# The hybrid mixers step on one Trainium2 core: two pauses of level four in the HGRN2 recurrence's place in the queue of jobs

## The chip, the core and the metric

The kernel runs on one core of one Trainium2 chip. A core has a matrix engine (TensorE, PE in the profile; PEld is its weight load), three engines for everything else (VectorE or DVE, ScalarE or ACT, GpSimd or POOL) and a queue that issues transfers (SyncE, SP). Each engine runs its own list of instructions in its own order; semaphores tie them together. Results of TensorE land in PSUM, which the others read.

The metric is the time of one execution on the device, in microseconds. The kernel before takes 1027.42 us, the median of three runs (1027.24 to 1028.08).

## The reference, cut to what matters

Two inputs, 512 sample tokens and 128 prompt tokens, go through one layer. The 640 tokens are normalised, multiplied by a wide matrix `w_in`, and the columns of the result feed four mixers side by side:

```python
h = rmsnorm(x, lw['norm1_g']) * (1.0 + sc1) + sh1
proj = h @ lw['w_in']
(a_x, a_b, a_c, b_q, b_ff, b_fb, b_i, b_g, c_q, c_k, c_v, d_u, d_v) = jnp.split(proj, IN_SPLITS, axis=-1)
y_a = a_b * dwconv3(a_c * a_x, lw['conv_a_w'], lw['conv_a_b'])
y_b, s_f, s_b = hgrn2_bidir(b_q, b_ff, b_fb, b_i, b_g, ...)
y_c = ...attention over a neighbourhood...
y_d = chunk_gmlp(d_u, d_v, ...)
merged = (g_a * (y_a @ lw['w_br_a']) + ... + g_d * (y_d @ lw['w_br_d']))
x = x + g1 * (merged @ lw['w_o'])
x = x + g2 * conv_ffn(rmsnorm(x, lw['norm2_g']) * (1.0 + sc2) + sh2, ...)
```

The change lies in `hgrn2_bidir`, a recurrence run forwards and backwards over the tokens. In one direction, with decay `f`, key `k`, value `v` and query `q`:

```python
decay = jnp.exp(jnp.where(tri, rel, -jnp.inf))
scores = jnp.einsum('bhctd,bhcsd,bhctsd->bhcts', q, k, decay)
o_intra = jnp.einsum('bhcts,bhcsv->bhctv', scores, v)
u = jnp.einsum('bhcsd,bhcsv->bhcdv', k * jnp.exp(cum_end - cum), v)
s_next = g_c[..., None] * s + u_c
o_inter = jnp.einsum('bhctd,bhcdv->bhctv', q * jnp.exp(cum), s_in)
```

## The kernel before

Features lie on the 128 partitions and the 640 tokens along the free axis. The projection by `w_in` is the backbone of the first third of the kernel. It goes section by section (the forget gates, q, i, g, dv, du, ck, cq, cv, ac, ax, ab), each in two tiles of 128 columns. One tile (`in_tile`, which calls `gemm`) is 48 matmuls of 128x320 in two halves of 8 groups; a group (one k) is three matmuls, because each product is made of a high and a low part. Each tile's weights are split into these parts by ScalarE (L323) and VectorE (L324) two tiles ahead.

The mixers' small work is put in between by a queue of jobs. It acts while the program is written out, not on the chip. A job is a generator; it issues instructions and yields a pause. A counter `now` stands for TensorE's time: each group of a projection tile adds 0.41 to it (`tick`), small products inside a job add their own estimate (`pe`), and after each tick every job that is due takes one step:

```python
def step(j):
    j[0] = now[0] + (next(j[1]) or 0.0) * j[2]
def tick(us):
    now[0] += us
    for j in list(jobs):
        if j[0] <= now[0]:
            step(j)
```

`j[0]` is the due time, `j[2]` a factor on the job's pauses: 1.3 for the recurrence, which starts when the q section is done. The list `HD` holds pauses of the jobs; `HD[1]` is 5. Python evaluates `now[0]` in `step` before it runs the job.

The order so written is TensorE's order in this region; the framework lays out the other engines' work around it from data dependencies and its own estimates, and sets all semaphores.

The recurrence (`hgrn`) doubles the length of the block in seven levels. At each of levels one to four it makes, for each half of the features (`par` 0 and 1), a burst of 40 small products (80 matmuls in the profile, since the operands are plain f32) into one bank of PSUM (L526). VectorE merges them under a mask (L531). After the first burst the job pauses (L537, 0.4); after the second it scales keys and queries for the next level (L545, L549), and pauses again (L550, `HD[1]`). At level four the merged scores are also copied to the large matrix `at` by ScalarE (L541). Level five has bursts of the same size and level six four smaller ones, and there ScalarE copies them (L535). Then follow, in the same job: the transposes of keys (`kt_load`, L565, L568), state updates (`upd`, L574, L585), outputs (L612 to L624), a pause for the norm, and five steps of last transposes (L635, L639).

Other jobs at work in this region: `ada_cols`, which makes the modulation's later columns on VectorE (L262), loads its weights by SyncE (L248), and has one transpose on TensorE after its eighth column (`gain_rows`, L291); `gmlp`, with five steps of 8 products (L673) and their scaling on VectorE (L678). All small products take their PSUM bank from a pool of four, `psm`.

Of the kernel before, what the change touches and what calls it, by code (L numbers as in the profile page):

```python
# [17 lines left out]
HD = [4, 5, 2.1, 7, 2.2, 1.4, 1.5, 5, 2.0, 2, 11]  # L18
# [49 lines left out]
def tile_step(ctx: ExitStack, tc: tile.TileContext, a: dict, outs: list, dbg=None):  # L68
# [21 lines left out]
    def pe(us):  # L90
        now[0] += us
# [38 lines left out]
    def pm():  # L130
        return psm.tile([P, 512], F32, tag="m", name=nm("m"))
# [315 lines left out]
    def hgrn():  # L447
# [13 lines left out]
        def along(x):  # L461

            m = pm()
            mv = m[:, 0:20].rearrange("p (r i) -> p i r", r=2)
            for i in range(10):
                mm(mv[:, i, :], x[:, i * P:(i + 1) * P], heads, start=True, stop=True)
                pe(0.22)
                yield 0.5
            return m
# [16 lines left out]
        def blk(x, B):  # L486
            return x.rearrange("p n t -> p (n t)").rearrange("p (n j i) -> p n j i", j=2, i=B)

        def keys(l):
            B = 1 << l  # L490
            kl = (he if l % 2 == 0 else hd)[:, 0:1280]
            klv = kl.rearrange("p (n j i) -> p n j i", j=2, i=B)
            vec.tensor_copy(klv[:, :, 0, :], blk(kk[:, 0], B)[:, :, 0, :])
            act(klv[:, :, 1, :], blk(kk[:, 1], B)[:, :, 1, :], AF.Copy)
            return kl
# [3 lines left out]
        for l in range(7):  # L499
            B = 1 << l  # L500
            e_, x_ = blk(kk[:, 0], B), blk(kk[:, 1], B)
            r_, p_ = blk(qq[:, 0], B), blk(qq[:, 1], B)
            f_, g_ = blk(ff[:, 0], B), blk(ff[:, 1], B)
            nb = 1280 // (2 * B)
            if l == 0:
                m = yield from along(near)
                vec.copy_predicated(nat, lmask[:, 0, :].unsqueeze(1).to_broadcast([P, 20, 32]), bc(m))

            W = 64 if l == 6 else 32
            ns = 320 // W  # L510
            for s0, par in ([(s_, r) for s_ in range(0, 10, ns) for r in range(2)] if l else ()):
                b = slice(64 * par, 64 * par + 64)
                m = pm()
                for i in range(s0, s0 + ns):
                    for g in range(P // W):
                        d, t0 = (0, W * g) if l < 5 else (1 - g % 2, W * (g ^ 1))
                        t0 += (i % 5) * P
                        k0 = i * P + W * g
                        rhs = qq[b, d, i // 5, t0:t0 + W]
                        if l < 5:  # L520
                            lhs = kl[b, k0:k0 + W]
                            rhs = bass.AP(rhs.tensor, rhs.offset,
                                          [list(rhs.ap[0]), [2 * B, 16 // B], [1280 + B, 2], [1, B]])
                        else:
                            lhs = f2(kk[:, g % 2])[b, k0:k0 + W]
                        mm(m[W * g:W * g + W, (i - s0) * W:(i - s0 + 1) * W], lhs, rhs,  # L526
                           start=True, stop=True, tile_position=(64 * par, W * g))
                    pe(0.18)
                mv = m[:, 0:ns * W].rearrange("p (i t) -> p i t", t=W)
                if l < 5:  # L530
                    vec.copy_predicated(near_at[:, par], lmask[:, l, :].unsqueeze(1).to_broadcast([P, 10, 32]), mv)  # L531
                else:
                    for g in range(P // W):
                        c = slice(W * g, W * g + W)
                        act(at[c, par, s0:s0 + ns, W * (g ^ 1):W * (g ^ 1) + W], mv[c], AF.Copy)  # L535
                if par == 0:
                    yield 0.4  # L537
            if l == 4:
                for g in range(4):
                    c = slice(32 * g, 32 * g + 32)  # L540
                    act(at[c, :, :, c].rearrange("p r i t -> p (r i) t"), nat[c], AF.Copy)  # L541
            ups = ((e_[:, :, 0, :], f_[:, :, 1, 0:1]), (x_[:, :, 1, :], g_[:, :, 0, 0:1]),
                   (p_[:, :, 1, :], f_[:, :, 0, 0:1]), (r_[:, :, 0, :], g_[:, :, 1, 0:1]))
            for i, (dst, mul) in enumerate(ups):
                vec.tensor_tensor(dst, dst, mul.to_broadcast([P, nb, B]), ALU.mult)  # L545
                if i == 1 and l < 4:
                    kl = keys(l + 1)
            fa = ff.rearrange("p d n t -> p (d n t)").rearrange("p (n j i) -> p n j i", j=2, i=B)
            vec.tensor_tensor(fa[:, :, 0, 0], fa[:, :, 0, 0], fa[:, :, 1, 0], ALU.mult)  # L549
            yield HD[1]  # L550
        vec.tensor_copy(tot, ff.rearrange("p d n (t s) -> p d n t s", s=P)[:, :, :, :, 0])
        R["tots"] = True

# [331 lines left out]

    SLACK = {"q": 1.3, "du": 1.4, "ax": 1.0, "cv": 1.1}
    starts = {"q": hgrn, "du": gmlp, "ax": conva, "cv": attn}

    def in_tile(sec, n, w):
# [1283 lines left out]
```

## Time and profile before

| | |
|---|---|
| median of three runs | 1027.42 us (1027.24 to 1028.08) |
| the profiled execution | 1028.79 us |
| its span, first to last instruction | 1026.9 us |
| TensorE busy | 1013.4 us (99%) |
| VectorE busy | 792.3 us (77%) |
| ScalarE busy | 535.5 us (52%) |
| mean granted TensorE clock | 0.996 |
| recurrence, levels one to six on TensorE (L526) | 110.5 to 157.3 us of the span |

Times in the profile count from the span's first instruction. The chain of waits follows the work that ended last back from the end: each of its rows has a start, a length and what it was; "issue" is time in which the engine waited for nothing that the profile shows. A count there can be below the number of matmuls issued, since neighbours that overlap are merged and a few records can be missing. In a row of the view by stretches stand the stretch, its length, the busy time and number of instructions of PE, PEld, DVE, ACT and POOL, the granted clock of TensorE, the share of the DMA engines and GB/s. In the list of waits: who waited, for whom, the total in us, how often, the longest. In the page's third part a row of a DMA queue has packets, MB, and share.

### The profile page before, as it was taken

The page shows a single profiled execution, that of the slowest core. Times are in us where ns is not written, and L with a number is a line of the kernel's source. Part 1 is how long each engine was busy: PE and PEld are TensorE (multiplying, and loading weights), DVE is VectorE, ACT ScalarE, POOL GpSimd, SP SyncE. Part 2 cuts the span into 40 slices and gives each one's busy share as a digit, 9 for nine tenths or more (in the row PEclk, how much of TensorE's full clock was granted, in tenths as well). Part 3 has the DMA queues.
Part 4 walks back from the last instruction along what each step waited for, and adds up shares of the span by engine and source line. Part 5 has one row for each costly group of instructions (what it writes and reads, how often), then busy time and mean ns, then how long its engine had stood idle before and what let it go on. Part 6 is the DMA issues. An engine that isn't in the chain of part 4 may idle for free.

```text
span 1026.9 us, 18833 instructions
## 1 busy us (share of the span) xinstructions
PE 1013.4 (99%) x7620; PEld 957.8 (93%) x7620; DVE 792.3 (77%) x1300; ACT 535.5 (52%) x927; POOL 106.2 (10%) x149
## 2 busy tenths in 40 slices
PE   8999999999999999999999999999999999999997
PEld 6899999999899999999998899999999999888886
DVE  6658889679965676767768879998888887797634
ACT  6642343444444444544544567777777776633332
POOL 1000010313100000000010111111112211001101
PEclk9999999999999999999999999999999999999999
DMA  9864333598562413323179584765555669974212
GB/s 354 319 220 127 125 108 121 137 270 268 121 205 78 137 69 103 127 79 103 41 276 359 200 333 109 192 167 150 149 150 149 156 161 274 366 248 149 89 35 103
DMA packets 55927, 177.87 MB, mean 173 GB/s; under 512 B 8192, under 2 KB 14624, under 8 KB 53280
## 3 DMA queue, kind: packets, MB, share of 16 engines
q1 hardware_dynamic: 45008, 140.60, 39.5%
q0 software_dynamic: 10832, 36.06, 14.7%
q8 instruction: 60, 0.98, 0.4%
q14 instruction: 27, 0.22, 0.1%
HBM read 134.93 MB, written 25.46 MB: 156 GB/s over the span
## 4 chain that ended last, share of the span: by engine, by line
PE 96%; DMA 1%; ACT 1%; DVE 1%; issue 1%; SPq 0%; POOL 0%; POOLq 0%; DVEq 0%; ACTq 0%
PE g L1464 19%; PE g L362 17%; PE m L1108 17%; PE g L1795 8%; PE m L1795 6%; PE g L1121 5%; PE m L1464 4%; PE m L1248 3%; PE g L920 2%; PE g L1248 2%; PE m L148 2%; PE g L148 1%; PE m L526 1%; PE m L1459 1%; DMA A<-in_w_ada_dram 1%; PE m L851 1%
## 5 line engine op out<-in xcount | busy, mean ns | idle before, releaser
L362 PE MATMUL g<-XH,w 128*128 128x320 f32 x704 | 171.9, 319 | 0.0
L362 PEld LDWEIGHTS g<-XH,w 128*128 128x128 f32 x704 | 121.6, 190 | 2.2 <-issue 1.2
L362 PE MATMUL g<-XL,w 128*128 128x320 f32 x352 | 109.8, 312 | 0.0
L362 PEld LDWEIGHTS g<-XL,w 128*128 128x128 f32 x352 | 66.9, 190 | 0.3 <-issue 0.2
L311 DVE TENSOR_TENSOR w<-raw,w 128x1024 fp32r<-128x1024 f32 x34 | 41.5, 1222 | 21.4 <-ACT w L310 15.2
L1108 PE MATMUL m<-XH,w 128*128 128x320 f32 x224 | 52.5, 309 | 0.0
L1795 PE MATMUL g<-w,XH 128*128 128x512 f32 (+1 forms) x216 | 47.6, 373 | 0.0
L310 ACT ACTIVATE w<-raw 128x1024 fp32r<-128x1024 f32 x34 | 35.7, 1050 | 21.3 <-PE g L1248 9.9
L1795 PEld LDWEIGHTS g<-w,XH 128*128 128x128 f32 x216 | 38.4, 188 | 7.6 <-ACT XH L1758 0.3
L148 DVE SCALAR_TENSOR_TENSOR X<-MG,p2t,X 128x641 f32<-128x641 f32 x44 | 38.9, 885 | 4.3 <-ACT X L148 3.4
L148 DVE SCALAR_TENSOR_TENSOR X<-X,p2t,X 128x641 f32<-128x641 f32 x44 | 38.9, 885 | 1.9 <-ACT X L148 1.0
L1795 PE MATMUL g<-w,XL 128*128 128x512 f32 (+1 forms) x180 | 39.8, 372 | 0.0
L148 ACT ACTIVATE w<-raw 128x1024 fp32r<-128x1024 f32 (+3 forms) x46 | 38.2, 850 | 2.9 <-DMA raw<-in_w_in_dram 2.0
L1795 PE MATMUL m<-w,XH 128*128 128x512 f32 (+1 forms) x180 | 39.7, 368 | 0.0
L1464 PE MATMUL g<-XL,w 128*128 128x320 f32 x240 | 38.6, 310 | 0.0
L1464 PE MATMUL g<-XL,C 128*128 128x320 f32 x240 | 38.4, 309 | 0.0
L1795 PEld LDWEIGHTS g<-w,XL 128*128 128x128 f32 x180 | 32.3, 188 | 6.5 <-DVE dt L1806 0.4
L1108 PEld LDWEIGHTS m<-XH,w 128*128 128x128 f32 x224 | 38.3, 188 | 0.0
L1464 PEld LDWEIGHTS g<-XL,w 128*128 128x128 f32 x240 | 36.0, 188 | 0.5 <-ACT MG L148 0.3
L1464 PEld LDWEIGHTS g<-XL,C 128*128 128x128 f32 x240 | 35.9, 188 | 0.4 <-ACT MG L148 0.4
L1795 PEld LDWEIGHTS m<-w,XH 128*128 128x128 f32 x180 | 31.3, 189 | 5.3
L1108 PE MATMUL m<-XL,w 128*128 128x320 f32 x112 | 34.6, 309 | 0.0
(546 smaller groups left out, 2764.5 us busy)
## 6 DMA issues: line engine op xcount, KB each, us to landing
raw<-in_w_up_dram SPq DMA_DIRECT2D x30, 512.0 KB, 5.2
raw<-in_w_gp_dram SPq DMA_DIRECT2D x21, 640.0 KB, 3.9
raw<-in_w_down_dram SPq DMA_DIRECT2D x22, 512.0 KB, 4.0
raw<-in_w_in_dram SPq DMA_DIRECT2D x19, 512.0 KB, 4.1
H<-in_w_adt_dram SPq DMA_DIRECT2D x16, 512.0 KB, 4.3
actd<-X POOLq DMA_DIRECT2D x22, 320.5 KB, 5.5
X<-in_w_adt_dram SPq DMA_DIRECT2D x10, 512.0 KB, 4.4
upd<-XL SPq DMA_DIRECT2D x4, 1280.0 KB, 6.5
```

The costliest lines, as they stand in the source:

```text
L148: r = f(*args, **kw)
L310: act(w[0], raw, AF.Copy)
L311: vec.tensor_tensor(w[1], raw, w[0].bitcast(F32), ALU.subtract)
L362: mm(o, w[:, h, k0 + k, :], r(k)[:, s], start=(k == 0 and i == 0), stop=(k == kt - 1 and i == 2))
L526: mm(m[W * g:W * g + W, (i - s0) * W:(i - s0 + 1) * W], lhs, rhs, start=True, stop=True, tile_position=(64 * par, W * g))
L851: mm(mo[64 * hh_:64 * hh_ + 64, 0:P], v, ptt[(u + hh_) % 3][:, j * P:(j + 1) * P], start=(j == 0), stop=(j == 2))
L920: mm(o, x(kx)[:, ts], w[:, h, k, :], start=(kx == 0 and i == 0), stop=(kx == 7 and i == 2))
L1108: mm(o, w[:, k, :], x[:, k, :], start=(first and k == 0 and j == 0), stop=(k == 3 and j == 2), skip_group_check=True)
L1121: mm(pb[:, c, 0:HC], w[:, h + k, :], y[:, x, k, s], start=(k == 0 and j == 0), stop=(k == 1 and j == 2))
L1248: mm(m, mh[k // 2][:, hx, k % 2, t * P:(t + 1) * P], wo[q][:, hw, k % 2, :], start=(k == 0 and i == 0), stop=(k == 7 and i == 2))
L1464: z = mm(o, w[:, k, :], x[:, k, :], start=(first and k == 0 and j == 0), stop=(k == 3 and j == 2), skip_group_check=True)
L1795: mm(acc[nh][t + c0 // 256][:, 0:c1 - c0], sl[k][hx][:, t * P:(t + 1) * P], w[:, hw, k, c0:c1], start=(kk_ == 0 and k == 0 and i == 0), st ...
```

## The change

At level four the pause after the first burst becomes 1.6, and the closing pause becomes 5 - 1.2 = 3.8. All other levels keep 0.4 and 5. No instruction is added, removed or altered in what it computes.

```diff
                 if par == 0:
-                    yield 0.4
+                    yield 1.6 if l == 4 else 0.4
...
             vec.tensor_tensor(fa[:, :, 0, 0], fa[:, :, 0, 0], fa[:, :, 1, 0], ALU.mult)
-            yield HD[1]
+            yield HD[1] - (1.2 if l == 4 else 0)
```

## The prediction

> **What bounds the kernel now.** I read the page's engine shares and instruction queue first, then the waits of TensorE, the chain of waits around the level, and a table of busy time by stretch.
>
> ```profile
> span 1026.9 us, 18833 instructions
> PE 1013.4 (99%) x7620; PEld 957.8 (93%) x7620; DVE 792.3 (77%) x1300; ACT 535.5 (52%) x927; POOL 106.2 (10%) x149
> q8 instruction: 60, 0.98, 0.4%
> ```
>
> TensorE (PE) is busy for 1013.4 of 1026.9 us, so another engine's order matters only where it makes PE wait. All PE waits of the kernel that the view lists:
>
> ```profile
> PE g L148 <- DVE F L148: 1.6, 1, 1.6
> PE m L148 <- DMA A<-in_w_ada_dram: 1.3, 2, 0.9
> PE m L526 <- issue: 1.1, 1, 1.1
> PE m L148 <- DVE X L148: 1.1, 4, 0.3
> PE m L1464 <- DVE w L148: 0.4, 1, 0.4
> PE m L1464 <- ACT MG L148: 0.3, 1, 0.3
> ```
>
> One of these, 1.1 us, lies in L526, the recurrence's bursts. The chain of waits from level three to the end of the recurrence's levels (start, length, what):
>
> ```profile
> 128.35 0.82 PE m L526 x58
> 129.17 5.47 PE g L362 x36
> 134.64 0.82 PE m L526 x58
> 135.46 0.21 PE m L291
> 135.67 0.44 PE g L362 x3
> 136.11 0.75 PE m L526 x54
> 136.86 1.14 issue
> 138.00 0.26 PE m L526 x7
> 138.26 7.01 PE g L362 x36
> 145.27 0.82 PE m L526 x58
> 146.09 0.64 PE g L362 x3
> 146.73 0.82 PE m L526 x58
> 147.55 5.47 PE g L362 x36
> 153.02 0.73 PE m L526 x20
> ```
>
> Level four is the pair at 134.64 and 136.11. Its second burst stops for 1.14 us near its end, where PE waits for nothing shown. Afterwards 36 projection matmuls take 7.01 us where the same 36 take 5.47 us after levels three and five: 1.54 us more. The stretches tell why (length, PE busy, ..., granted clock):
>
> ```profile
> 135.00:138.40 3.40, 2.26 (x137) 1.88 (x126) 3.02 (x8) 0.27 (x1) 0.00 (x0) 1.00 0.20 41
> 138.40:141.80 3.40, 3.40 (x14) 3.40 (x14) 3.37 (x7) 2.90 (x4) 0.00 (x0) 0.50 0.35 125
> 141.80:205.00 63.20, 63.20 (x682) 60.34 (x681) 51.18 (x106) 26.64 (x60) 11.86 (x11) 1.00 0.41 121
> ```
>
> For 3.4 us after the stop the granted clock is 0.50. So in this execution the stop costs 1.14 + 1.54 = 2.68 us. From 141.80 to 205.00 PE has no idle time and the full clock.
>
> That stop looks like an instruction fetch: 7620 matmuls and 7620 weight loads over 60 packets are 254 instructions a packet, and over 134.0 to 136.8 us the DMA view has one packet only, one of these:
>
> ```profile
> DMA packets 1, 0.02 MB, mean 6 GB/s; under 512 B 0, under 2 KB 0, under 8 KB 0
> q8 instruction: 1, 0.02, 2.2%
> ```
>
> A level's two bursts are 80 matmuls each, so 320 instructions: more than one packet. In level four, two packet ends are only 2 us apart: the stop comes 146 instructions into the second burst (73 matmuls), so the end before it lies 254 - 146 - 8 = 100 instructions from the close of the first burst.
>
> [...]
>
> **The change part by part.** The edit moves no instruction by itself: it alters two due times in the queue of jobs that decides where the recurrence's steps are put among the projection's matmuls. A step's due time is the counter before the step plus pause times 1.3 (the slack of the job started at "q"). A burst adds 10 x 0.18 = 1.8 to the counter; each group of three projection matmuls adds 0.41 and then lets due jobs run.
>
> 1. The pause of 1.6. Before: due 0.4 x 1.3 = 0.52 after the first burst began. After: 1.6 x 1.3 = 2.08. But the burst itself moves the counter by 1.8, and the first chance to run is at 1.8 + 0.41 = 2.21 (level four has the gain transpose there too, 0.11 more). Both due times are past by then. The second burst stays where it is, after three matmuls. The row 135.67 (x3) is this rule at work, and so is 146.09. So the program up to the end of level four's second burst is unaltered, and with it the packet ends: the stop of 1.14 us and the slow 3.4 us stay. Change: 0.
>
> 2. The closing pause. It counts from the start of the second burst. Before: 5 x 1.3 = 6.5; less 1.8, 4.7 remain, which is 12 groups (12 x 0.41 = 4.92): the 36 matmuls of rows 129.17, 138.26 and 147.55. After: 3.8 x 1.3 = 4.94; less 1.8, 3.14 remain: 8 groups (3.28). Level five's first burst comes 4 groups, 12 matmuls, earlier. A group is 0.44 us, from
>
> ```profile
> 323.45 1.76 PE g L1121 x12
> ```
>
> (0.147 us each), so 1.76 us: 145.27 becomes about 143.5. It pulls everything that follows in this job: level six, the state updates, the outputs.
>
> Does its data come in time? Level five reads what level four's updates leave, and level six what level five's leave (timeline of VectorE):
>
> ```profile
> 138.73 1.55 DVE L545 TENSOR_TENSOR C<-C,A 128x640 f32<-128x640 f32 x2
> 140.19 0.30 DVE L549 TENSOR_TENSOR A<-A 128x80 f32<-128x80 f32 x1
> 149.57 1.56 DVE L545 TENSOR_TENSOR C<-C,A 128x640 f32<-128x640 f32 x2
> 160.56 0.60 DVE L678 SCALAR_TENSOR_TENSOR X<-m,cst,G 128x128 f32<-128x128 f32 x2
> 161.08 1.22 DVE L262 SCALAR_TENSOR_TENSOR junk<-X,S 128x1024 bf16<-128x1024 f32 x1
> 162.22 1.13 DVE L678 SCALAR_TENSOR_TENSOR X<-m,cst,G 128x128 f32<-128x128 f32 x4
> ```
>
> For level five they end at 140.5: 3 us of cover are left. For level six they end at 151.1 against a burst at 153.0; its distance from level five's second burst stays 12 groups, and these updates now stand ahead of a weight split that VectorE did first. Cover about 1.9 us, taken as enough; if one 1.22 us operation (row 161.08) still gets ahead, it is used up and nothing more.
>
> New packet ends: counted from the stop, 14 instructions of level four are left, then 24 matmuls (48), 160 of level five's first burst and 6, so the next end is 26 instructions into its second burst, about 145.1 us, some 7 us after the stop; one more 254 on is the start of level six's second burst, about 152.6. No two come within 2 us. Change: 0.
>
> 3. Breaks in the stream. 36 matmuls take 5.47 us after a burst, against 36 x 0.147 = 5.28: each return to the projection costs 0.19 us. Stepping the queue by hand with the two due times, the recurrence's and the gMLP's steps from here on interrupt the projection at 22 places instead of 21 (before the last transposes, whose 5 stay): level six's later bursts no longer share a place with the gMLP's first two steps, while the first state transpose now shares one with its last. Change: +0.19 us, between 0 and +0.4 if one place more or less falls together.
>
> 4. The far end. The chain's last transposes run during the last cv tile, 2.46 counter units earlier; attention and the rest start only when that tile is done. From tile ac on the order is as before. Change: 0.
>
> Semaphores, DMA issues and the amount of work on each engine are unaltered. SyncE's queue keeps its loads; the weight loads released by VectorE's splits may move by the length of a few operations, with two tiles (over 10 us) of cover.
>
> Sum: 0 + 0 + 0.19 + 0 = +0.2 us, a span of 1027.1. The profiled execution took 1028.79, 1.37 above the runs' median of 1027.42; against the median the forecast is **1027.6 us**. 0.2% (2.05 us) is about the least that a measurement of this kernel tells from no change.
>
> **The rivals.**
>
> (B) The pause does separate the bursts. That would be so if the due time counted from the end of the burst: 2.08 is 6 groups, 18 matmuls. Then the second burst starts some 5 x 0.44 = 2.2 us later, its packet has come, and the stop and the slow stretch both go: 1027.6 - 2.68 = 1024.9. Against it: by that count 0.52 would need two groups, 6 matmuls, and all rows have 3.
>
> [...]
>
> (C) Slower. PSUM's pool for small results has four banks. The first state transposes (two banks) now fall in the same place as the gMLP's last product, about 161.0 us, where before they came at 163.1. If VectorE keeps its order, banks come free at 161.2, 162.7 and 163.3 (rows 160.56 and 162.22, whose four operations empty two banks). The third result would wait from about 161.4 to 163.3, 1.9 us, with PE's queue behind it; and a stop of 1.14 us had 1.54 us of slow clock behind it. 1027.6 + 1.9 + 1.5 = 1031.0. It decides only if VectorE has not emptied them sooner; for that speaks that level six's updates, 3 us of work, now run about 2 us earlier, and that PE's order is laid out around expected waits. Without the slow clock it is 1029.5.
>
> (D) The stop stays, but the slow stretch doesn't follow in the timed runs, since it need not fall on the same moment in each: 1027.6 - 1.5 = 1026.1. The three runs differ by 0.84 us, so at least part of this is open.
>
> **How the numbers follow.** Forecast 0.66, B 0.06, C 0.12, D 0.16. B is faster by over 0.2%, C slower; the forecast and D are within it: faster 0.06, same 0.82, slower 0.12. The range runs from D less 0.3 to C without the slow clock: 1025.8 to 1029.6; it leaves out B and the dearer part of C, under 2 in 10.
>
> **What would show it.** Right: in the changed kernel's chain, three matmuls between level four's bursts, an "issue" piece of about 1.1 us in the second, then 24 instead of 36 matmuls before level five; a stretch at half clock after it; PE without idle time from 142 to 205 us. Wrong: eighteen matmuls between the bursts and no issue piece (B); a PE wait on L565, L574 or L673 near 161 us with VectorE as releaser (C); a new issue piece in levels five or six, which would mean that my count of packet ends is off; or any wait beyond tile ac.

## The result, and the profile after

The changed kernel takes **1031.98 us** (median of six runs, 1030.85 to 1032.18) against 1027.71 us (1027.24 to 1028.93, six runs) for the kernel before beside it: 1.0035 times as long, with a 95% interval of 1.0025 to 1.0045. It is slower by 4.3 us. The forecast was 1027.6 us, with a range of 1025.8 to 1029.6.

The profiled execution after took 1031.26 us, 2.5 us more than the profiled execution before (1028.79). Its page begins:

```profile
span 1029.5 us, 18834 instructions
PE 1013.3 (98%) x7620; PEld 956.8 (93%) x7620; DVE 793.2 (77%) x1300; ACT 535.8 (52%) x927; POOL 105.9 (10%) x149
```

TensorE's work is unaltered (1013.3 against 1013.4 us); what grew is its idle time. The list of its waits, and below it the chain of waits around levels four and five (both of after):

```profile
PE m L526 <- issue: 1.5, 1, 1.5
PE m L834 <- DVE X L831: 1.3, 2, 1.1
PE m L851 <- DVE B L836: 1.3, 1, 1.3
```

```profile
136.05 0.44 PE g L362 x3
136.49 0.75 PE m L526 x54
137.24 1.54 issue
138.78 0.26 PE m L526 x7
139.05 3.71 PE g L362 x24
142.76 0.82 PE m L526 x58
143.58 0.64 PE g L362 x3
144.22 0.82 PE m L526 x62
145.04 5.47 PE g L362 x36
```

The chain is what steps 1 and 2 foretold: three matmuls between level four's bursts, the stop in the second one, 24 matmuls in place of 36 before level five, and 36 again before level six. Only the slow stretch behind the stop is missing: the 24 matmuls take 3.71 us, and the granted clock from 138 to 144 us is 1.00. The new entries are the two waits on L834 and L851, which stand far behind the recurrence, in attention. Two stretches of each kernel show how much they are worth (columns as before: the stretch, its length, then the busy time of PE, PEld, DVE, ACT and POOL). Before:

```profile
205.00:250.00 45.00, 45.00 (x343) 42.31 (x341) 36.91 (x84) 20.85 (x44) 10.37 (x13) 1.00 0.92 279
250.00:320.00 70.00, 70.00 (x505) 65.22 (x504) 55.10 (x104) 32.77 (x51) 7.85 (x10) 1.00 0.51 148
```

After:

```profile
141.80:205.00 63.20, 63.20 (x678) 59.17 (x676) 51.67 (x109) 27.52 (x61) 12.52 (x11) 1.00 0.43 128
205.00:250.00 45.00, 44.76 (x339) 42.18 (x338) 33.91 (x76) 20.64 (x44) 8.10 (x11) 1.00 0.87 239
250.00:320.00 70.00, 67.64 (x490) 62.87 (x489) 57.15 (x107) 32.55 (x49) 9.86 (x12) 1.00 0.54 159
```

From 141.8 to 205 us PE has no idle time in either kernel. From 205 to 320 us it has none before and 0.24 + 2.36 = 2.60 us after, the sum of the two waits. VectorE did 3 us less than before in the first of these stretches and 2 us more in the second: some of its work has moved back.

Which work, the timeline of VectorE tells. Before:

```profile
192.56 1.22 DVE L262 SCALAR_TENSOR_TENSOR junk<-H,S 128x1024 bf16<-128x1024 f32 x1
200.90 1.22 DVE L262 SCALAR_TENSOR_TENSOR H<-H,S 128x1024 f32<-128x1024 f32 x1
267.38 1.21 DVE L262 SCALAR_TENSOR_TENSOR A<-A,S 128x1024 f32<-128x1024 f32 x1
275.38 1.49 DVE L650 TENSOR_TENSOR A<-MG,A 128x1280 fp32r<-128x1280 f32 x1
```

After:

```profile
194.54 2.03 DVE L630 TENSOR_TENSOR MG<-MG,hss 128x1280 f32<-128x1280 f32 x1 [3.43 <-POOL hss L305]
213.39 1.22 DVE L262 SCALAR_TENSOR_TENSOR junk<-H,S 128x1024 bf16<-128x1024 f32 x1
215.47 1.22 DVE L262 SCALAR_TENSOR_TENSOR H<-H,S 128x1024 f32<-128x1024 f32 x1
277.34 1.22 DVE L262 SCALAR_TENSOR_TENSOR A<-A,S 128x1024 f32<-128x1024 f32 x1
281.43 1.48 DVE L650 TENSOR_TENSOR A<-MG,A 128x1280 fp32r<-128x1280 f32 x1
```

A column of the modulation is two products of 1.22 us on VectorE (L262). The pair on H that lay at 192.6 and 200.9 us, beside a wait for GpSimd, comes at 213.4 and 215.5; the last column ends 10 us later (278.6 against 268.6), and the split on L650 behind it starts 6 us later. This pair is column 32. Every column behind it is late too; column 31 itself starts its second product no later (197.7 against 199.2 us).

That these columns hold PE up shows in the chain of waits of after. In attention it leaves PE and runs through VectorE; this is its piece before the 1.1 us wait on L834:

```profile
256.68 1.14 DVE junk L262 x2
257.82 0.07 DVE ast L830
257.89 0.51 DVE MG L692
258.41 0.34 DVE X L831
258.75 0.14 issue
```

A product of a column, 1.14 us of the chain, stands right before the scaling (L831) that PE waits for.

The reason stands in three lines of the columns' own job that I did not quote before the prediction (after each column, L275 to L277):

```python
            yield gap
            while "hgrn_out" in R and "hgrn_done" not in R:
                yield 1
```

Once the recurrence has written its outputs ("hgrn_out", L626), and until its last transposes are done ("hgrn_done", L643), no new column is begun. Counter values of the queue of jobs, written out as the two programs are made:

```
                                       before    after
recurrence sets "hgrn_out"             137.20   134.74
column 31 would begin                  136.79   136.79
column 31 begins                       136.79   153.06
column 32 begins                       154.70   159.27
column 39 begins                       202.09   208.80
```

Before, column 31 slips past the hold by 0.41, one group of the projection. After, the outputs are 2.46 earlier, so the same column meets the hold and waits for 16 units; the eight columns behind it shift too.

### The profile page after: what moved, and what is told of

Its sections match the earlier page's. It is cut to its first block, busy times and chain, and to the rows that moved or that the text cites. A ratio compares the mean times of both kernels' runs of the same rounds, so it can differ in the third digit from the quotient of the medians.

```text
span 1029.5 us, 18834 instructions
## 1 busy us (share of the span) xinstructions
PE 1013.3 (98%) x7620; PEld 956.8 (93%) x7620; DVE 793.2 (77%) x1300; ACT 535.8 (52%) x927; POOL 105.9 (10%) x149
## 4 chain that ended last, share of the span: by engine, by line
PE 91%; DVE 3%; DMA 2%; issue 1%; ACT 1%; SPq 0%; POOL 0%; POOLq 0%; DVEq 0%; ACTq 0%
PE g L1464 19%; PE m L1108 17%; PE g L362 14%; PE g L1795 8%; PE m L1795 6%; PE g L1121 5%; PE m L1464 4%; PE m L1248 3%; PE g L920 2%; PE g L1248 2%; PE m L148 2%; PE g L148 1%; PE m L526 1%; PE m L1459 1%; DMA A<-in_w_ada_dram 1%
## 5 line engine op out<-in xcount | busy, mean ns | idle before, releaser
L1795 PE MATMUL g<-w,XH 128*128 128x512 f32 (+1 forms) x216 | 47.6, 373 | 0.0
L1795 PEld LDWEIGHTS g<-w,XH 128*128 128x128 f32 x216 | 38.4, 188 | 7.6 <-ACT XH L1758 0.3
L1795 PE MATMUL g<-w,XL 128*128 128x512 f32 (+1 forms) x180 | 39.8, 372 | 0.0
L1795 PE MATMUL m<-w,XH 128*128 128x512 f32 (+1 forms) x180 | 39.7, 368 | 0.0
L1795 PEld LDWEIGHTS g<-w,XL 128*128 128x128 f32 x180 | 32.3, 188 | 6.4 <-DVE dt L1806 0.2
L1795 PEld LDWEIGHTS m<-w,XH 128*128 128x128 f32 x180 | 31.3, 189 | 5.3
L323 ACT ACTIVATE w<-raw 128x1024 fp32r<-128x1024 f32 (+1 forms) x22 | 24.3, 1104 | 21.3 <-PE g L362 8.5
```

The source lines that it names most:

```text
L323: high = lambda: act(w[:, 0], raw, AF.Copy)
L1795: mm(acc[nh][t + c0 // 256][:, 0:c1 - c0], sl[k][hx][:, t * P:(t + 1) * P], w[:, hw, k, c0:c1], start=(kk_ == 0 and k == 0 and i == 0), st ...
```

## The experiments

Two theories. **T1**: the loss is made by the columns, which the earlier outputs hold back into attention, where VectorE ends last. **T2**: the recurrence's earlier steps cost it themselves. A "code block" in the expectations is what one packet of the profile's queue "q8 instruction" brings; the profile before has 60 of them. Each run stands beside executions of the kernel before on the same chip; their median is given with it. Those medians move (1027.66 to 1028.55 in four sets); most of the longer executions have a lower mean clock (in the set of 1027.84, 0.996 or 0.997 in the eleven from 1028.37 us up, 0.997 to 0.999 in the other twelve). So it is with the half-clock stretch behind the stop, which comes in some executions and not in others: the profiled execution before has it and a mean clock of 0.996, the one after hasn't and has 0.998.

**1. Column 31 let through, nothing else** (after_pass31).

```diff
-            while "hgrn_out" in R and "hgrn_done" not in R:
+            while f != 30 and "hgrn_out" in R and "hgrn_done" not in R:
```

> The changed kernel, but modulation column 31 no longer meets the hold that waits for the recurrence's outputs; the recurrence's own times stay as changed (24 matmuls before level five). T1 (the loss is one modulation column, 2 x 1.22 us of VectorE, that moved from the projection into attention, where VectorE ends last): the PE waits on L834 and L851 (1.3 + 1.3 us) go or fall under 0.5 us, and the time is back at 1027 to 1029 us, within 0.2% of before. T2 (the earlier levels five and six, their breaks, their code blocks and the clock cost the time themselves): nothing comes back, 1031 to 1032.5 us.

Measured: 1038.97 us (1037.37 to 1040.96) against 1027.84; 1.0104 times, 1.0089 to 1.0119. Far from either theory. Now "hgrn_done" is early too, so the columns behind 31 are released before their places of before and VectorE meets one whose load hasn't landed. Waits of PE, and one row of VectorE's timeline:

```profile
PE m L834 <- DVE X L831: 3.5, 1, 3.5
PE g L362 <- ACT gt L958: 2.8, 1, 2.8
```

```profile
252.75 1.23 DVE L262 SCALAR_TENSOR_TENSOR junk<-H,S 128x1024 bf16<-128x1024 f32 x1 [3.51 <-DMA H<-in_w_adt_dram]
```

VectorE stands 3.51 us behind a load, and PE 3.5 us behind VectorE. The two waits of PE, 6.3 us, aren't the whole excess: behind each the profile has a half-clock stretch (granted clock 0.50 from 261 to 263 and from 295 to 297 us; 0.95 on the mean from 250 to 285 and from 285 to 320 us, where the profile before has 1.00). T1 in its narrow form, "one column too late", fell: a column too early costs more. What was left of it is that each column's place against attention sets the time.

**2. Column 31 held in the kernel before** (before_hold31).

```diff
-            while "hgrn_out" in R and "hgrn_done" not in R:
+            while ("hgrn_out" in R or f == 30) and "hgrn_done" not in R:
```

> The kernel before, with the recurrence untouched, but column 31 held back until the recurrence's outputs are done, as the changed kernel does by accident. T1: slower by 2 to 4.5 us (1029.5 to 1032), with new PE waits for VectorE between 225 and 320 us. T2: within 0.2% of before, no such waits.

Measured: 1034.21 us (1030.42 to 1036.16) against 1027.84; 1.0053 times, 1.0037 to 1.0069. Slower, as T1 said, and by more: here the hold ends 2.46 units later than in the changed kernel, and the profiled execution, the longest of the six, has half-clock stretches behind the stop (mean granted clock 0.79 from 135 to 143 us, as in the profile before) and in attention (0.50 from 292 to 295 us; 0.95 on the mean from 285 to 320 us). The recurrence is as before, so T2 can't account for it.

**3. The outputs back in their place, levels five and six early** (after_l6_back, level six's pause longer; after_out_back, the pause behind the last state update longer).

```diff
-            yield HD[1] - (1.2 if l == 4 else 0)
+            yield HD[1] - {4: 1.2, 6: -1.9}.get(l, 0)
```

```diff
-            yield 1
+            yield 2.9 if f == 4 else 1
```

> The changed kernel with level six's closing pause longer by 1.9: levels four to six as changed, but the state updates and the outputs are back at the place that they had before, and so is column 31. T1: 1026.5 to 1029, no PE wait in attention. T2 in the form that level five's early place costs (breaks, code blocks, slow clock between 135 and 160 us): 1030.5 to 1032.5; in the form that only the state updates' early place costs it is back at before too, which the run without the hold tells apart.

> The changed kernel with the pause behind the last state update at 2.9 in place of 1: levels five and six and the state updates as early as changed, the outputs and with them the modulation columns at the places of before. If the outputs' early place is what costs (by the columns, and by the loads ahead of a column's load): 1028 to 1029.5 us, only the added breaks over before, no PE wait between 205 and 320 us. If the earlier levels and state updates cost: 1030.5 to 1032.

Measured: 1028.32 us against 1027.84 (1.0005, 0.9997 to 1.0014), and 1028.61 us against 1027.66 (1.0009, 0.9999 to 1.0019). In both, the columns have the counter values of before. Attention in after_out_back, by the same stretches; PE waits for nothing there:

```profile
205.00:250.00 45.00, 45.00 (x342) 42.23 (x341) 36.91 (x83) 21.19 (x44) 9.27 (x12) 1.00 0.92 271
250.00:320.00 70.00, 70.00 (x501) 65.15 (x502) 55.08 (x104) 32.43 (x51) 7.87 (x10) 1.00 0.50 147
```

Both lie in the first case's range of their expectations. So by the medians the earlier levels and state updates cost 0.5 to 0.95 us (the intervals reach from no change to 2 us), and the rest of the 4.3 hangs on the outputs' place. The 0.95 fits a count of places where PE's rows leave the projection, from level four's first burst to attention's first transpose: 33 before, 37 in the changed kernel and in after_out_back, 35 in after_l6_back; four more at the forecast's 0.19 us are 0.76. One of them in the chain of waits of after, where the state updates share with no other job any more:

```profile
161.79 0.59 PE m L673 x8
162.37 0.64 PE m L574 x4
163.01 0.72 PE g L362 x5
163.74 0.45 PE m L574 x4
```

Before, one place held all eight (the chain there: "165.55 0.89 PE m L574 x8").

**4. Columns moved, the recurrence left** (before_cols_after), **and the recurrence early, columns put back** (after_cols_before).

```diff
-            while "hgrn_out" in R and "hgrn_done" not in R:
-                yield 1
+            if f == 30:
+                yield 16
```

```diff
-            while "hgrn_out" in R and "hgrn_done" not in R:
-                yield 1
+            while f != 30 and "hgrn_out" in R and "hgrn_done" not in R: yield 1
+            if f == 31: yield 2.3
```

> The kernel before, recurrence untouched, with the modulation columns put at the counter values of the changed kernel (column 31 from 153.03 in place of 136.79). T1, mended: slower by 2.5 to 4.5 us (1030.3 to 1032.3), with the changed kernel's PE waits on L834 and L851. T2: within 0.2% of before.

> The changed kernel (24 matmuls before level five, state updates and outputs early), with the modulation columns put at the counter values that they have in the kernel before: column 31 passes the hold, and column 32 starts 2.3 after the hold's end. The first run without the hold fell (1039 us): there the columns after 31 came earlier than before, ahead of their loads. T1, mended (where each column falls against attention's steps sets the time; the earlier levels cost nothing): 1027 to 1029 us, no PE wait for VectorE or loads between 205 and 320 us. T2 (the earlier levels and state updates cost by themselves, whatever the columns do): 1030.5 to 1032.5.

Measured: 1029.42 us (1028.67 to 1030.89) for the first and 1030.18 us (1027.72 to 1032.34) for the second against 1028.55; ratios 1.0006 (0.9995 to 1.0018) and 1.0012 (1.0000 to 1.0025). By the medians both missed T1's ranges: the first is within 0.2% of before, as T2 said, and the second lies between the two ranges. The profiled executions speak for T1: from attention's first transpose (L736) to the end, the first falls back by 2.4 us against the same instructions of the profile before, and PE waits 1.3 us on L851; the second loses nothing there. But the median of before stood high in this set (15 of 35 executions had a mean clock of 0.996 or less, none of the first kernel's twelve), and the second kernel's executions spread over 4.6 us. A base without the stop was needed.

**5. Level four's bursts really apart** (apart, apart_again: 15 matmuls between them, level five in its place).

```diff
-                    yield 0.4
+                    yield 2.9 if l == 4 else 0.4
...
-            yield HD[1]
+            yield HD[1] - (1.25 if l == 4 else 0)
```

> The kernel before with the pause between level four's bursts at 2.9 and its closing pause shorter by 1.25: 15 matmuls between the bursts and level five in the place of before. If the stop in the second burst is a code block that comes late and the half clock follows from it: no issue piece in the chain near 137 us, no stretch below full clock, 1.1 to 2.7 us faster than before (1025 to 1026.6). If the stop moves with the burst or the clock falls for another reason: within 0.2% of before.

> The kernel with level four's bursts 15 matmuls apart, once more, as the base for the three runs beside it: without the stop and without the half clock near 140 us their times should lie closer together. Expected 1025.8 to 1027.5 us, faster than before by 1 to 2.5 us.

Measured: 1026.45 us against 1027.84 (0.9983, 0.9975 to 0.9992) and 1026.30 us against 1028.12 (0.9979, 0.9969 to 0.9989). This is faster than both kernels. Chain of waits of apart_again:

```profile
134.58 0.82 PE m L526 x58
135.40 0.21 PE m L291
135.61 2.20 PE g L362 x15
137.81 0.82 PE m L526 x58
138.63 3.71 PE g L362 x24
```

No "issue" piece, and the 24 matmuls take 3.71 us, at a granted clock of 1.00 (134 to 205 us). So the stop goes when the bursts lie apart; that it is an instruction fetch stays my estimate from the count of packets, and no run shows it. The profiled execution of apart had a half-clock stretch elsewhere (granted clock 0.50 from 15 to 18 us, 0.83 on the mean from 10 to 20 us), so a mean clock alone doesn't tell where a stretch lies.

**6. The same three edits on that base** (apart_cols_after: columns as in the changed kernel; apart_early: level five 12 matmuls earlier, by a closing pause shorter by 2.45 in place of 1.25; apart_early_cols: that with the columns put back as in 4).

> That base with the modulation columns at the counter values of the changed kernel, its recurrence untouched. T1 (the columns' places against attention's steps cost 2.4 us, as the two profiles with and without them show): 1028.2 to 1029.6 us, PE waits on L851 and L834. T2 (the recurrence's earlier steps cost the time): as the base, 1025.8 to 1027.5.

> That base with level four's closing pause shorter by another 1.2, as in the changed kernel: level five 12 matmuls earlier, and with it column 31 meets the hold. T1 with four more breaks in the projection (0.8 us) and the columns (2.4 us): 3.2 us over the base, 1029 to 1030.7. T2: the same 3 us, but from the recurrence alone; the next run tells.

> The run beside it with the columns put back at the places of before (column 31 passes the hold, column 32 starts 2.3 after its end). T1: only the four breaks are left, 0.8 us over the base: 1026.6 to 1028.3, no PE wait in attention. T2: 1029 to 1030.7, as without the columns' move.

Measured, against the base's 1026.30: **1028.34** (1027.69 to 1028.85), **1029.97** (1029.39 to 1032.09) and **1029.61** (1027.74 to 1033.98). The first is the cleanest test of the study: the recurrence keeps its places, and the columns' places cost 2.0 us; ten of the base's twelve executions are shorter than all eleven of this kernel. Its waits of PE between 205 and 320 us, of which the base has none:

```profile
PE m L851 <- DVE B L836: 1.3, 1, 1.3
PE m L834 <- DVE X L831: 0.2, 1, 0.2
```

The second is 3.7 over the base, as both theories said. Here only 12 matmuls lie between level four and level five, where the changed kernel has 24, and the profiled execution has a new stop, in level five's second burst, which takes 2.71 us in place of the base's 0.82:

```profile
141.31 0.90 PE m L526 x63
142.21 1.03 issue
143.25 0.78 PE m L526 x52
```

The third missed T1's range (1026.6 to 1028.3) by 1.3 us and lies in T2's: with the outputs early, putting the columns back returns 0.4 us by the medians, not the 2.0 that moving them cost. One part of this is the spacing, which the changed kernel doesn't have: the same burst of level five is slow here too.

```profile
141.89 1.49 PE m L526 x98
```

From level four's first burst to L736 the profiled execution takes 1.2 us more than the base's, 0.7 of it in this burst. Breaks can't be the reason: by the count of 3, the base has 33 places and this kernel 34, one more and not the four that the expectation took over. This execution was, at 1028.41, the second fastest of twelve, so this kernel was profiled twice more, and after_cols_before once more.

> A second look at the kernel with bursts apart, level five early and columns put back. If a column's load that lands late is the cause: in an execution of 1029 us or more VectorE waits over 3 us for a column's load between 225 and 250 us and PE waits for VectorE behind it; an execution near 1028 has neither.

> A third look at the same kernel, with the same expectation: if it falls on an execution of 1029 us or more, VectorE waits over 3 us for a column's load there.

> A second look at the changed kernel with the columns put back. The first, 1027.9 us, had no loss in attention; eight of its twelve executions took 1030 us or more. Expected of one of these: VectorE waits over 2 us for a column's load between 225 and 250 us. If it shows none and the time went before 211 us, the load is not the cause.

They took 1030.34, 1027.73 and 1030.19 us. (Of after_cols_before's twelve, seven took 1030 us or more, not eight.) The first two are one program, and differ in how long VectorE waits for one column's load between 211 and 250 us. In the 1030.34, this wait, and two of PE's:

```profile
DVE junk L262 <- DMA A<-in_w_adt_dram: 3.1, 1, 3.1
```

```profile
PE m L851 <- DVE B L836: 0.5, 1, 0.5
PE g L1795 <- DVE dt L1806: 1.0, 1, 1.0
```

In the 1027.73:

```profile
DVE junk L262 <- DMA A<-in_w_adt_dram: 1.3, 1, 1.3
```

From L736 to 320 us the one falls back by 1.3 us, the other by nothing; 1.2 us more go in the last stage (L1795), which is no part of this. The execution of 1028.41 stands between them, with a wait of 2.6 us and 0.8 us lost. In after_cols_before_b the wait is 1.9 us (a little under the 2 expected), 0.9 us are lost in attention, and the half-clock stretch, which the first profile of this kernel lacked, is there (mean granted clock from 135 to 143 us: 0.79 against 1.00). With the outputs early, then, a column put back stands near the landing of its load, and some executions pay for it. At 1.3 us and less, this doesn't fill the third kernel's 3.3 us over the base, even with the 1.2 us before attention.

**7. Column 32 left out** (after_no32, before_no32): its two products are replaced by two small fills, so this modulation column is not computed.

```diff
-                    vec.scalar_tensor_tensor(raw if v else junk, raw, 1.0, cr[:, v], ALU.mult, ALU.mult,
-                                             accum_out=ar[:, v:v + 1]))
+                    vec.memset(ar[:, v:v + 1], 0.0) if f == 32 else vec.scalar_tensor_tensor(
+                        raw if v else junk, raw, 1.0, cr[:, v], ALU.mult, ALU.mult, accum_out=ar[:, v:v + 1]))
```

> The changed kernel with column 32's two products (2 x 1.22 us of VectorE, at 213 to 217 us there) left out and replaced by two small fills; its loads stay, and modulation column 32 is not computed. T1: VectorE ends last in attention, so most of the loss comes back: 1027.5 to 1029.5. T3 (not VectorE's work but the later loads of the columns in SP's queue cost): little comes back, 1030.5 to 1032.5.

> The kernel before with the same column 32 left out, as a control: there its two products lie before 203 us, where VectorE has time. T1: within 0.1% of before, 1026.8 to 1028.8. If leaving out 2.4 us of VectorE is worth time wherever it lies: 1025 to 1026.

Measured: 1030.60 us (1029.25 to 1032.93; 1.0021, 1.0009 to 1.0033) and 1029.05 us (1028.17 to 1030.46; 1.0005, 0.9995 to 1.0015), both against 1028.55. The changed kernel is 2.05 us over before in place of 4.3, but the two figures stand on different sets; from its own 1031.98 it is 1.4 us. Its 1030.60 misses T1's range and lies at the lower end of T3's. In the profile the wait on L834 is gone and the 1.4 us on L851 remain; the columns behind 32 stay late. So column 32's work is a part of the loss at most, and the run doesn't part VectorE's work from the later loads. In the kernel before, 2.4 us less of VectorE are worth nothing (the ratio is as T1 said, the time just above its range): there they were hidden, as the control was to show. The edit also shifts the framework's order of some other VectorE work, so its tenths mean little.

## Why the prediction was wrong

**Step 1** (pause of 1.6: 0) was right about the order: three matmuls between the bursts, the stop in place. It also kept the slow stretch, which the profiled execution after doesn't have. **Step 2** (level five 12 matmuls earlier, data in time, no new stop) was right in each part.

**Step 3** (breaks, +0.19 us, at most 0.4) had the right mechanism and the wrong size. The rows show four more places, not one; after_out_back, which has these and the columns as before, measured +0.95 us, and the profiles below give 0.7.

**Step 4** failed: "From tile ac on the order is as before. Change: 0." I saw that the chain's last part moves by 2.46 counter units and looked at who waits for its results. I did not look at who waits for its flags. A job with no data from the recurrence reads two of them, and its column 31 begins 16 units later, those behind it 4 to 7; from there on the order was not as before. The columns issue their own loads, so SyncE's queue changed its order too, where the prediction says that it keeps its loads. This is worth 2.0 us in the medians (apart_cols_after) and 2.6 in the changed kernel's profile. "Any wait beyond tile ac" was named as a sign of failure, and it came.

By the medians 0.95 and 2.0 leave 1.3 of the 4.3 us. The two profiles add up better. From the start of level four's first burst to attention's first transpose (L736) the execution before took 76.72 us and the one after 76.31. Less the stops (1.14 and 1.54) and the slow stretch (1.54, before only) this is 74.04 and 74.77: 0.7 us for the breaks. From L736 to the end it is 2.6 us. Together that makes 3.3, and the two executions after with a mean clock of 0.998 (1030.85 and 1031.26) lie 3.1 and 3.6 us above the median of before. The other four, at 0.996, took 1031.94 to 1032.18 us: probably the half clock, but no profile of one of them was taken.

So it is shown that the outputs' early place makes most of the loss (put back, 0.5 to 0.95 of the 4.3 are left) and that the columns' shift alone costs 2.0. What stays open is why putting the columns back, with the outputs early, returns so little by the medians: 1030.18 us in one set, and 1029.61 against 1029.97 in another.

**Rival B** described another change, and its price was of the right order: with the bursts really apart the kernel gained 1.4 and 1.8 us, where 2.68 was the price in an execution with the slow stretch. **Rival C** fell: no PE wait near 161 us. That its 1031.0 lies near the measured 1031.98 is chance. **Rival D** was half right: of 23 executions of before beside the first set, the eleven that took 1028.37 us or more had a mean clock of 0.996 or 0.997, the other twelve 0.997 to 0.999; the two groups' medians differ by 1.6 us, against the 1.54 worked out from the chain. The profiled execution after had its stop and no such stretch.

## What to carry to other kernels

In a queue of jobs with flags, moving one job's pause moves its flags. List every place that reads a flag which the moved step sets, in all jobs, and compare its margin with the shift: here the margin was 0.41 units and the shift 2.46. Where a program's order is made by such a queue, write out the order of every engine to the end, not only the moved job's; and test two effects that come together on a base where each can be had alone.

## What the hardware showed unexpectedly

The same stop, in level four's second burst, lasted 1.05 to 1.54 us in the eleven profiled executions that have it; in five of them, before and after among these, the timeline has it before matmul 74 of the 80. Its length doesn't decide on the half clock behind it: four have the slow stretch (stops of 1.14, 1.18, 1.47 and 1.54 us), seven don't (1.05 to 1.54 us, the changed kernel's among them). From 135 to 143 us the mean granted clock is 0.79 in each of the four and 1.00 in each of the seven. In the profile before, the stretch is the 3.4 us at 0.50 from 138.4 us on, behind a stop of 1.14 us. What decides whether it comes, no run here shows.
